# Sixteen starting places for the split weights of an input projection

## The chip, the cores and the metric

The kernel runs on one core of a Trainium2 chip. The metric is the device time of one execution, in microseconds (us). A core has a matrix engine (PE, whose weight loads the profile lists apart as PEld), three engines for elementwise work (DVE, ACT and POOL) and SP, which here only issues DMA transfers. Each engine takes its instructions in the order in which the program lists them and waits on semaphores for the others. Data for the engines lies in SBUF, a memory of 128 partitions, and a matrix product is summed in PSUM.

## The reference

One layer of a decoder trunk on x of 512 tokens by 4096 features, float32:

```python
h = rms_norm(x, norm_g)
q, k, v, z = split(h @ w_in + b_in)        # 4096, 512, 512 and 4096 columns
o = banded_sink_attention(q, k, v, sinks)  # 64 query heads, 8 key heads of 64, window of 128 tokens
x = x + (o * silu(z)) @ w_out + b_out
return rms_norm(x, final_g)
```

## The kernel before

Every float32 operand of a projection is split into two numbers, a high part that is rounded to a shorter form (`fp32r`) and the rest, and a product takes three matmuls: high by high, high by rest, rest by high. ACT makes the high part (`whi`) with a cast, and DVE the rest (`wlo`) with a subtraction (`split`, lines 141 to 145).

There are three stages.

1. The value projection. x is loaded, scaled and split into `xhi` and `xlo`, which stay in SBUF, and for each of 32 blocks of 128 features four blocks of tokens are multiplied with 512 columns of the value weights. x is the operand that is loaded into PE as weights here, `whi` and `wlo` stream past it. The last `LAST` = 3 blocks are held back and taken one token block after another, so that three pairs of split weights are in use at once until the end of the stage.
2. The input projection, with the attention laid between its matmuls. 68 column tiles (`NT`) of 128 output columns follow each other: per pair of key groups one tile of keys (name `None`), and then per group eight of `TILES`. A column tile has 8 chunks (`kc`), a chunk 4 blocks (`j`), a block 3 matmuls, so 96 matmuls of 512 columns. Here 128 columns of `whi` or `wlo` are loaded into PE and `xhi` or `xlo` stream past. One chunk is one buffer of `whi` and one of `wlo`, 512 columns each; `load_w` brings two chunks in one DMA of 512 KB. After each chunk, `tick` lets due pieces of attention follow: scores (`ps`), then the transposes of the probabilities (`pt`), then the product with the values (`po`). A *quad* is the attention of four query heads in four token blocks; there are 16 quads, each with four blocks of tokens.
3. The output projection, in 8 blocks of 512 columns, where the split gated output `gs` is loaded into PE and `whi` and `wlo` stream past it, and then the final norm.

`whi` and `wlo` have `WB` = 4 buffers each in all three stages. The cast of a chunk waits until PE has done with the chunk four before. PE's instructions are kept in the order in which the code gives them (`mm`, `tr`); those of the other engines are put into an order by a scheduler when the program is built.

What lies where in a partition: the buffers of `whi` and `wlo` are 2,048 bytes long, those of `xhi` and `xlo` 8,192 bytes with a block of 2,048 bytes each, and every one of them begins 128 bytes past a multiple of 512. Since a block of weights within a buffer begins at a multiple of 512 bytes too, the weights of any matmul of a projection lie at a multiple of 512 bytes from the x that streams past (distance 0 from here on, for all such multiples). `gs` of the output projection lies at distance 0 from `whi` as well. The buffers of the attention (`q`, `kh`, `vv`, `vw`, `wh`) begin 64 bytes past a multiple of 512.

## Time and profile before

| | |
|---|---|
| median of 2 runs | 2407.35 us (2406.91 to 2407.78) |
| the profiled execution | 2406.92 us |
| its span, first to last instruction | 2405.2 us |
| PE busy | 2392.2 us, 99% of the span |
| DVE, ACT, POOL busy | 58%, 41%, 14% |
| clock granted to PE, mean | 0.998 of full speed |

A row of the profile names the source line, the engine, the operation, and `out<-in` by the program's names. `acc<-xhi,wlo` on PE is a matmul into `acc` with x streaming and `wlo` loaded. A matmul row gives the start, which is measured, and a length, whose end is modelled; matmuls overlap, so that the spacing of starts is what a matmul costs.

### The profile page before, as it was taken

The numbers are of one execution on the slowest core, as the hardware profiler recorded it, in microseconds if no ns is written. First come the engines' busy times: TensorE is split into PE (matmuls) and PEld (weight loads), VectorE is DVE, ScalarE is ACT, GpSimd is POOL, SyncE is SP. The second block draws the span as 40 slices with busy tenths as digits, with TensorE's granted clock in tenths as the row PEclk, the third lists the DMA queues.
The fourth block names the chain that finished last, engine by engine and source line by source line (L and its number), as shares of the span: only waits on it lengthen the run. The fifth ranks groups of instructions, "written<-read, shape, count | busy, mean of one in ns | idle before, by whom it ended". The sixth has DMA issues, their size and how long they took to land.

```text
span 2405.2 us, 30234 instructions
## 1 busy us (share of the span) xinstructions
PE 2392.2 (99%) x10988; PEld 1991.1 (83%) x10988; DVE 1403.9 (58%) x2502; ACT 985.0 (41%) x2129; POOL 340.7 (14%) x472
## 2 busy tenths in 40 slices
PE   9999999999999999999999999999999999999998
PEld 7888888888888888888888888888888888888886
DVE  5446656555575564656656466565764664665565
ACT  6433433434343342433433334334444444444444
POOL 1101111121020121102102011111210110110110
PEclk9999999999999999999999999999999999999999
DMA  9633233233333323333233332334633433333334
GB/s 343 189 93 102 85 110 97 88 112 86 103 99 92 102 89 110 92 94 105 85 105 104 92 99 86 112 97 128 228 123 97 125 123 100 124 124 97 122 119 184
DMA packets 81077, 280.45 MB, mean 117 GB/s; under 512 B 10080, under 2 KB 10080, under 8 KB 80928
## 3 DMA queue, kind: packets, MB, share of 16 engines
q1 hardware_dynamic: 70176, 243.37, 32.7%
q0 software_dynamic: 10608, 34.88, 4.4%
q8 instruction: 86, 1.41, 0.2%
q14 instruction: 63, 0.52, 0.1%
q10 hardware_dynamic: 144, 0.28, 0.0%
HBM read 259.61 MB, written 18.88 MB: 116 GB/s over the span
## 4 chain that ended last, share of the span: by engine, by line
PE 99%; DMA 0%; DVE 0%; POOL 0%; ACT 0%; DVEq 0%; issue 0%; POOLq 0%
PE acc L112 94%; PE ps L112 2%; PE po L112 2%; PE pt L115 1%; DMA xraw<-in_x 0%; POOL wl L425 0%; POOL wh L425 0%; DVE y L688 0%; ACT xhi L241 0%; ACT y L712 0%; DVE xb L711 0%; DVEq L794 0%; DVE y L692 0%; POOL ww L425 0%; DVE y L678 0%
## 5 line engine op out<-in xcount | busy, mean ns | idle before, releaser
L144 DVE TENSOR_TENSOR wlo<-raw,whi 128x512 fp32r<-128x512 f32 x822 | 587.4, 716 | 760.2 <-ACT whi L143 751.5
L143 ACT CAST whi<-raw 128x512 fp32r<-128x512 f32 x821 | 510.7, 622 | 1204.1 <-PE acc L112 1148.3
L112 PE MATMUL acc<-xhi,wlo 128*128 128x512 f32 x2176 | 849.2, 390 | 0.0
L112 PE MATMUL acc<-xhi,whi 128*128 128x512 f32 x2176 | 848.6, 390 | 0.0
L112 PE MATMUL acc<-xlo,whi 128*128 128x512 f32 x2176 | 848.3, 390 | 0.0
L112 PE MATMUL acc<-whi,gs 128*128 128x512 f32 x1968 | 606.0, 389 | 0.0
L112 PEld LDWEIGHTS acc<-xhi,wlo 128*128 128x128 f32 x2176 | 408.4, 188 | 85.8
L112 PEld LDWEIGHTS acc<-xhi,whi 128*128 128x128 f32 x2176 | 409.1, 188 | 81.1
L112 PEld LDWEIGHTS acc<-xlo,whi 128*128 128x128 f32 x2176 | 408.4, 188 | 81.4
L112 PEld LDWEIGHTS acc<-whi,gs 128*128 128x128 f32 x1968 | 369.4, 188 | 76.7
L112 PE MATMUL acc<-wlo,gs 128*128 128x512 f32 x984 | 382.8, 389 | 0.0
L112 PEld LDWEIGHTS acc<-wlo,gs 128*128 128x128 f32 x984 | 184.7, 188 | 38.4
L144 DVE TENSOR_TENSOR gs<-g,gs 128x512 fp32r<-128x512 f32 x256 | 186.8, 770 | 0.7 <-ACT gs L143 0.7
L425 POOL TENSOR_SCALAR_AFFINE_SELECT ww<-wh 64x512 fp32r<-64x512 f32 x64 | 41.7, 651 | 881.7 <-ACT wh L421 881.7
L143 ACT CAST gs<-g 128x512 fp32r<-128x512 f32 x256 | 145.7, 616 | 1.7 <-PE acc L112 1.7
L497 DVE RECIPROCAL e<-e 128x128 f32<-128x128 f32 x128 | 120.6, 944 | 0.5
L399 ACT ACTIVATE prob<-ps,nm 128x128 f32<-128x128 f32 x256 | 90.4, 364 | 74.2 <-DVE nm L390 73.0
L704 POOL DMA_DIRECT2D xb<-in_x x32 | 17.3, 541 | 504.6 <-DVE y L714 430.8
L474 ACT COPY ot<-po 64x256 f32<-64x256 f32 x128 | 46.9, 367 | 56.8 <-DVE o L475 41.2
L475 DVE TENSOR_TENSOR o<-po,ot 64x256 f32<-64x256 f32 x128 | 52.8, 412 | 20.4 <-ACT ot L474 19.8
L348 DVE SCALAR_TENSOR_TENSOR q<-tmp,bcol,q 64x512 fp32r<-64x512 f32 x64 | 58.6, 916 | 7.2 <-ACT q L347 6.2
L274 DVE TENSOR_TENSOR tmp<-acc,rbc 128x512 f32<-128x512 f32 x37 | 25.6, 691 | 57.6 <-PE acc L112 57.6
(125 smaller groups left out, 1629.3 us busy)
## 6 DMA issues: line engine op xcount, KB each, us to landing
raw<-in_w_in SPq DMA_DIRECT2D x272, 512.0 KB, 3.6
raw<-in_w_out SPq DMA_DIRECT2D x128, 512.0 KB, 3.6
row<-in_x POOLq DMA_DIRECT2D x16, 512.0 KB, 6.5
gT<-o POOLq DMA_DIRECT2D x32, 256.0 KB, 2.3
g<-gT SPq DMA_DIRECT2D x16, 512.0 KB, 6.3
xb<-in_x POOLq DMA_DIRECT2D x32, 256.0 KB, 3.6
xraw<-in_xT SPq DMA_DIRECT2D x15, 512.0 KB, 7.1
raw<-in_w_v SPq DMA_DIRECT2D x15, 512.0 KB, 6.4
```

The source lines that it names most:

```text
L112: tc.keep_in_program_order(nc.tensor.matmul(*a, **k))
L115: tc.keep_in_program_order(nc.tensor.transpose(*a, **k))
L143: copy(hi, src),
L144: nc.vector.tensor_tensor(lo, src, hi.bitcast(F32), op=ALU.subtract),
L274: nc.vector.tensor_tensor(t, acc, rbc, op=ALU.mult)
L348: nc.vector.scalar_tensor_tensor(q2[other, :, h, :], tv[own], b[own], q2[own, :, h, :].bitcast(F32), op0=ALU.add, op1=ALU.subtract,)
L399: nc.scalar.activation(pr[:, u, a, :], ps[:, u, a, 0:P], AF.Exp, bias=nm[:, u, a:a + 1], scale=SCALE, accum_out=den[:, u, a:a + 1],)
L425: nc.gpsimd.affine_select(out=out, in_=src.bitcast(F32), fill=0.0, pattern=[[0, 8], [1 if own else -1, QH]], compare_op=ALU.is_ge if own e ...
L474: nc.scalar.copy(ot[own], pq[other, :, :, h, :])
L475: nc.vector.tensor_tensor(ov[own], pq[own, :, :, h, :], ot[own], op=ALU.add)
L497: nc.vector.reciprocal(c, c)
L704: nc.gpsimd.dma_start(xb, x[tb * P:(tb + 1) * P, cs])
```

## The change

The buffers of `whi` and `wlo` become longer by 128 columns (2,560 bytes), and each column tile but the last uses 512 columns that begin at one of sixteen places in them: 0, 4, 8, 12, 16, 24, and so on to 96 and 112 columns, in turn from tile to tile. In bytes the distance from x becomes 0, 16, 32, 48, 64, 96, 128, then by steps of 32 to 384, and 448, beyond a multiple of 512. The stages of the value projection and of the output projection, and the last column tile, keep place 0. So that the longer buffers fit, there are three of each in place of four, in all stages.

```diff
-WB = 4
+WB = 3
+
+PLACES = (0, 4, 8, 12, 16, 24, 32, 40, 48, 56, 64, 72, 80, 88, 96, 112)
...
+    place = [0]
...
     def split_w(raw, j, copy=nc.scalar.copy):
-        hi = wpool.tile([P, CW], F32R, name="whi", tag="whi", bufs=WB)
-        lo = wpool.tile([P, CW], F32R, name="wlo", tag="wlo", bufs=WB)
+        hi, lo = (
+            wpool.tile([P, CW + P], F32R, name=n, tag=n, bufs=WB)[:, place[0]:place[0] + CW]
+            for n in ("whi", "wlo")
+        )
         latest[1:] = split(raw[:, j], hi, lo, copy)
         return hi, lo
...
         for t, (g_, name) in enumerate(order):
             assert t == tile_no(g_, name)
+            place[0] = PLACES[t % len(PLACES)] if t < NT - 1 else 0
```

PE's instructions stand in the same order before and after. On the other engines the scheduler puts some of them elsewhere, because it reckons with three buffers. Lines of the new kernel are 2 to 7 further down.

On ACT, at the end of the value projection, the casts of the first chunks of the input projection stand ahead of a cast of the values, `vv`, that needs `vf`, which comes back from memory. Before:

```order
L241 ACTIVATE xhi_776<-xraw,gcol 128x512
L143 CAST whi<-raw 128x512
L241 ACTIVATE xhi_776<-xraw,gcol 128x512
L143 CAST whi<-raw 128x512 x6
L329 CAST vv<-vf 128x4x64
L143 CAST whi<-raw 128x512 x9
L316 ACTIVATE kh<-kf,bk 128x512
```

And now:

```order
L247 ACTIVATE xhi_776<-xraw,gcol 128x512
L145 CAST whi<-raw 128x512
L247 ACTIVATE xhi_776<-xraw,gcol 128x512
L145 CAST whi<-raw 128x512 x5
L335 CAST vv<-vf 128x4x64
L145 CAST whi<-raw 128x512 x8
L322 ACTIVATE kh<-kf,bk 128x512
```

Five casts of chunks stand ahead of `vv` in place of six: chunk 5 of the first column tile is now cast behind it.

On DVE, in the first quad, around the third of its four token blocks: `wl` is the rest of the transposed probabilities (which POOL then masks for PE), `e` a part of the gate's reciprocal, `o` a piece of attention output. Before:

```order
L408 TENSOR_SCALAR prob<-prob,den 128x128 x4
L144 TENSOR_TENSOR wlo<-raw,whi 128x512
L497 RECIPROCAL e<-e 128x128
L144 TENSOR_TENSOR wlo<-raw,whi 128x512
L497 RECIPROCAL e<-e 128x128
L475 TENSOR_TENSOR o<-po,ot 64x2x2x64
L144 TENSOR_TENSOR wlo<-raw,whi 128x512
L497 RECIPROCAL e<-e 128x128
L475 TENSOR_TENSOR o<-po,ot 64x2x2x64
L383 COPY_PREDICATED ps<-mask,ps 128x4x64
L422 TENSOR_TENSOR wl<-pt,wh 128x512
```

And now:

```order
L414 TENSOR_SCALAR prob<-prob,den 128x128 x4
L146 TENSOR_TENSOR wlo<-raw,whi 128x512 x2
L503 RECIPROCAL e<-e 128x128
L481 TENSOR_TENSOR o<-po,ot 64x2x2x64 x2
L146 TENSOR_TENSOR wlo<-raw,whi 128x512
L503 RECIPROCAL e<-e 128x128
L428 TENSOR_TENSOR wl<-pt,wh 128x512
L389 COPY_PREDICATED ps<-mask,ps 128x4x64
```

One reciprocal and the masking of the next scores, which stood ahead of `wl`, stand behind it now.

## Rows read from the trace of the kernel before

**Rows 1.** The page: busy time of the engines, their share and instructions.

```profile
PE 2392.2 (99%) x10988; PEld 1991.1 (83%) x10988; DVE 1403.9 (58%) x2502; ACT 985.0 (41%) x2129; POOL 340.7 (14%) x472
```

**Rows 2.** All waits of PE: for whom, us in total, times, longest.

```profile
PE idle L112 <- DVE zero L191: 1.3, 1, 1.3
PE po L112 <- POOL wl L425: 0.4, 1, 0.4
PE acc L112 <- ACT xhi L241: 0.3, 1, 0.3
```

**Rows 3.** Chain that ended last: the output projection (start us, us, what).

```profile
1697.77 696.38 PE acc L112 x3072
```

**Rows 4.** Timeline of PE and of its weight loads, plain column tile (start us, us).

```profile
500.55 0.39 PE L112 MATMUL acc<-xhi,wlo 128*128 128x512 f32 x1
500.55 0.19 PEld L112 LDWEIGHTS acc<-xhi,whi 128*128 128x128 f32 x1
500.78 0.39 PE L112 MATMUL acc<-xhi,whi 128*128 128x512 f32 x1
...
503.27 0.39 PE L112 MATMUL acc<-xhi,wlo 128*128 128x512 f32 x1
```

**Rows 5.** Timeline of PE, the last warm-up matmuls on 16-bit zeros.

```profile
4.23 0.81 PE L112 MATMUL idle<-zero 128*128 128x512 bf16 x3
4.88 0.59 PE L112 MATMUL idle<-zero 128*128 128x512 bf16 x2
```

**Rows 6.** Timeline of PE, first matmuls of a chunk behind a block of scores.

```profile
164.36 0.39 PE L112 MATMUL acc<-xhi,whi 128*128 128x512 f32 x1
...
165.06 0.39 PE L112 MATMUL acc<-xhi,whi 128*128 128x512 f32 x1
...
166.67 0.39 PE L112 MATMUL acc<-xlo,whi 128*128 128x512 f32 x1
...
167.12 0.39 PE L112 MATMUL acc<-xhi,whi 128*128 128x512 f32 x1
```

**Rows 7.** Timelines of PE and PEld, last matmul of a chunk ahead of scores.

```profile
163.46 0.39 PE L112 MATMUL acc<-xhi,wlo 128*128 128x512 f32 x1
163.46 0.41 PEld L112 LDWEIGHTS ps<-kh,q 128*128 128x128 f32 x2
163.68 0.30 PE L112 MATMUL ps<-kh,q 128*128 128x64 f32 x2
```

**Rows 8.** The page: groups of line 143 and 144 (mean ns, idle before, releaser).

```profile
L144 DVE TENSOR_TENSOR wlo<-raw,whi 128x512 fp32r<-128x512 f32 x822 | 587.4, 716 | 760.2 <-ACT whi L143 751.5
L143 ACT CAST whi<-raw 128x512 fp32r<-128x512 f32 x821 | 510.7, 622 | 1204.1 <-PE acc L112 1148.3
```

**Rows 9.** Timelines at the start of the input projection: PE, ACT, DVE.

```profile
92.96 0.39 PE L112 MATMUL acc<-xhi,whi 128*128 128x512 f32 x1
...
98.38 0.62 ACT L143 CAST whi<-raw 128x512 fp32r<-128x512 f32 x1 [2.10 <-PE acc L112]
105.02 0.41 ACT L329 CAST vv<-vf 128x256 fp32r<-128x256 f32 x1 [6.01 <-DMA vf<-vd]
105.33 1.83 ACT L143 CAST whi<-raw 128x512 fp32r<-128x512 f32 x3
109.26 0.62 ACT L143 CAST whi<-raw 128x512 fp32r<-128x512 f32 x1 [2.10 <-PE acc L112]
...
105.98 3.58 DVE L144 TENSOR_TENSOR wlo<-raw,whi 128x512 fp32r<-128x512 f32 x3
```

**Rows 10.** Timelines in a quad, third token block: DVE, POOL, PE.

```profile
288.72 0.94 DVE L497 RECIPROCAL e<-e 128x128 f32<-128x128 f32 x1
...
290.62 0.69 DVE L422 TENSOR_TENSOR wl<-pt,wh 128x512 fp32r<-128x512 f32 x1
...
292.71 1.17 POOL L425 TENSOR_SCALAR_AFFINE_SELECT wl<-wl 64x512 fp32r<-64x512 f32 x1
...
294.30 0.28 PE L112 MATMUL po<-wl,vv 128*128 128x256 f32 x1
```

## The prediction

> **What bounds the kernel now.** I began with the page: PE is busy for 99% of the span, no other engine for more than 58% [rows 1]. Busy alone proves little, since matmuls overlap, so I read PE's waits next: it waited three times, for 2.0 us in all [rows 2]. Nothing that feeds PE is late, and a change can only move the time through the cost of a matmul or by making PE wait where it doesn't now.

> The cost of a matmul is the spacing of starts. In a plain column tile, with no attention in it, twelve matmuls take 503.27 - 500.55 = 2.72 us, 226.7 ns each [rows 4]; over the whole output projection it is 696.38 / 3072 = 226.7 ns [rows 3]. The weights of the next matmul begin to load when the present one begins to stream (both at 500.55) and take 0.19 us [rows 4], so they are ready before it ends: the load is hidden, as far as time goes. Yet 226.7 ns isn't the least that 512 columns can take here. The last warm-up matmuls, also of 512 columns, but of 16-bit numbers, started (4.88 - 4.23) / 3 = 217 ns apart [rows 5]. So each matmul in fp32r carries some 10 ns more. Whether this has to do with where weights and x lie is what the change depends on.

> **The distances.** The input projection has 68 x 96 = 6528 matmuls. The place is 0 in tiles 0, 16, 32, 48, 64 and the last, so 62 tiles or 5952 matmuls get another distance. Between them the distances differ only below 512 bytes, and there every projection now has distance 0; the trace of before can't show the spacing at 16 or 32 bytes. It has one neighbouring case. The last matmul of a chunk ahead of a block of scores streams x while the weights of the scores are loaded, and these (`q`) begin 64 bytes past a multiple of 512 where x begins 128 past: the distance is -64, the same as 448, one of the sixteen. The load starts with that matmul (163.46), and the next matmul starts 163.68 - 163.46 = 0.22 us after it [rows 7], as at distance 0 to the resolution of the row. So one of the fifteen new places costs what place 0 costs, by this row.

> From both sides the cost of the other places is bounded by rows of other matmuls of this shape. Below: the warm-up's 217 ns, that is 10 ns less. Above: right behind a block of scores, where x and weights are at distance 0, the matmuls do not start 226.7 ns apart at once. From 164.36 to 166.67 there are ten, 231 ns each, the first three (to 165.06) 233 ns each; then two more to 167.12 take 0.45 us, which is the usual spacing again [rows 6]. The same instruction on the same addresses can thus cost some ns more, by how it meets the work ahead of it. I take 0, because the row with another distance [rows 7] is nearer to the question than rows with another type or another past. Both ends go into the range.

> [...]

> **Three buffers in place of four.** ACT spends most of its idle time ahead of a cast waiting for PE, that is for a free buffer [rows 8]. A cast now starts when the chunk four before is done, and three chunks of 12 x 226.7 ns = 2.72 us pass until its own turn, 8.16 us; with cast and subtraction (0.62 and 0.72 us [rows 8]) some 6.8 us are left, plus two matmuls for `wlo`. With three buffers the lead is 2.72 us shorter and 4 us are left. That hides it nearly everywhere. I looked for the places where something other than the buffer delays a chunk, and found two that matter.

> The first is the start of the input projection. ACT stands at `vv` until 105.02, when `vf` has come back from memory, after 6.01 us of idle time [rows 9]. Six chunks (0 to 5) were cast ahead of it; the order now has five there, because a sixth buffer isn't free yet. So chunk 5 is the first behind `vv`: cast from 105.33 to 105.95, and its subtraction, the first of three that start at 105.98 and take 3.58 us, ends at about 107.2 [rows 9]. PE begins chunk 5 at 92.96 + 5 x 2.72 = 106.56 and needs `wlo` two matmuls later, at 107.0. So PE waits some 0.2 us, once. If `vf` lands a microsecond later than it did, it waits 1.2 us. The hold of three blocks at the end of the value projection, with all three buffers taken, costs less: the first of them is free six matmuls (1.36 us) before the stage ends, and a cast of 0.62 us needs no more.

> The second is the third token block of each quad. POOL ends the mask of `wl` at 293.88, and PE uses it at 294.30: 0.42 us to spare [rows 10], in each of 16 quads. That mask waits for `wl` on DVE at 290.62, behind reciprocals of 0.94 us. In the new order `wl` stands ahead of one reciprocal and a masking that it stood behind, so the margin should rather grow. If a later `wlo` pushes it back by one reciprocal instead, PE waits 0.94 - 0.42 = 0.5 us in each quad, 8 us in all.

> What else moves is free of cost: SP's loads of w_in wait for raw buffers that come free a chunk later, and there are three of these with two chunks each, so loads still run six chunks ahead of casts. PE's own order is unchanged. Longer buffers change no instruction's size, and the 4 us of lead hide it if casts into odd places take longer.

> **The sum.** Profiled execution 2406.92 us (span 2405.2), 0 for the distances, 0.2 for chunk 5, 0 for the quads: 2407.1. The profiled execution is 0.4 under the median of the runs shown, so **2407.5 us**. About 2% (48 us) is what a measurement of this kernel can tell from no change.

> **Rivals.**

> *The distance frees the 10 ns* (faster). The load of the next weights and the streaming x would be in each other's way at distance 0, and at other distances not. For it: the 10 ns that fp32r matmuls carry, exactly the same in all plain stretches, all of which are at distance 0 [rows 3, 4]. Against it: distance -64 shows the usual 0.22 us [rows 7]. Price: 5952 x (226.7 - 217) = 58 us if all places gain, 2350; half of that, 2378, if half do.

> *The distance costs more* (slower). The places would shift the moment at which weights and x meet, as a block of scores does, and the spacing would stay where it is only passing now. For it: the spacing behind scores is not that of the steady run [rows 6], so something in PE depends on the moment. Against it: it comes back to 226.7 within ten matmuls by itself. Price: 5952 x (231 - 226.7) = 26 us, 2433; with 233 ns, 37 us, 2445. It decides from any place on at which a whole tile runs above 21.8 us (96 x 226.7 ns).

> *Three buffers are too few* (slower). The quads wait 0.5 us each and the start 1.2: 2416. For it: the 0.42 us of margin. Against it: the new order on DVE.

> That the change doesn't do what it says can be left aside: all buffers lie at the same remainder of 512, so each tile has one distance throughout.

> **How the numbers follow.** No effect of the distance, and at most a microsecond of waits (2406 to 2410): 0.66. Distance frees time, in whole or in part: 0.13. Distance costs time: 0.15. Three buffers too few: 0.06. The range: 2390 to 2435. Below it lies the first rival where it gains more than 3 ns per matmul (17 us), which I put at 0.09 of its 0.13; above it the second where it costs more than its mean price, 0.06. Faster by over 2% (under 2359) needs 8 ns of the 10 in every place: 0.05. Slower by over 2% (over 2455) needs 235 ns, more than any row for long: 0.05. Within 2%: 0.90.

> **What the profile of the changed kernel would show.** If I am right, every plain column tile takes 21.8 us whatever its place, and matmul starts are 0.227 us apart in each; PE's waits stay under 4 us, with one new one, for chunk 5 of the first tile. If a rival is right, the tiles differ by place, and those that share a place (16 tiles apart) agree. I would be wrong above all if places of 16 or 32 bytes, of which no row tells anything, run at another spacing than those of 64.

## The result, and the profile after

The changed kernel takes 2437.15 us (median of 2 runs, 2436.59 to 2437.72) against 2407.35: 1.0124 times as long, 95% interval 1.008 to 1.0167. The forecast was 2407.5 us with a range up to 2435. The time lies 2 us above the range and beside the price of the second rival (2433, or 2445). Its profiled execution took 2436.59 us, with a span of 2434.6 us where it was 2405.2.

The page, busy time of the engines, answers to [rows 1]: PE has 29.5 us more, the other engines nothing that could account for it.

```profile
PE 2421.7 (99%) x10988; PEld 1993.6 (82%) x10988; DVE 1404.8 (58%) x2502; ACT 982.2 (40%) x2129; POOL 334.0 (14%) x472
```

All waits of PE (us in total, times, longest), against [rows 2]: three, for 1.8 us in all. Waits of PE's weight loads are not in this view; two places where they are new, for 0.9 and 0.6 us, are described further down.

```profile
PE idle L114 <- DVE zero L197: 1.3, 1, 1.3
PE po L114 <- POOL wl L431: 0.3, 1, 0.3
PE acc L114 <- DVE part L662: 0.2, 1, 0.2
```

So the matmuls themselves cost more. Which ones is read from the page's groups of lines (busy us, mean ns of one, idle before): those that stream x past the weights have a longer modelled length than before, 395 ns in place of 390, and those of the output projection, with the same shape and type, have the same as before. Before:

```profile
L112 PE MATMUL acc<-xhi,whi 128*128 128x512 f32 x2176 | 848.6, 390 | 0.0
...
L112 PE MATMUL acc<-whi,gs 128*128 128x512 f32 x1968 | 606.0, 389 | 0.0
```

And now:

```profile
L114 PE MATMUL acc<-xhi,whi 128*128 128x512 f32 x2176 | 858.7, 395 | 0.0
...
L114 PE MATMUL acc<-whi,gs 128*128 128x512 f32 x1968 | 606.2, 389 | 0.0
```

The chain that ended last, at the start of the output projection, gives the stage (start us, us, what), to compare with [rows 3]:

```profile
1726.74 607.25 PE acc L114 x2679
```

The timeline of PE at the start of the input projection (93.56), and at the two ends of the first chunk of two column tiles, at 256 bytes (330.98) and at 32 bytes (523.57), answers to [rows 4]:

```profile
93.56 0.39 PE L114 MATMUL acc<-xhi,whi 128*128 128x512 f32 x1
...
330.98 0.39 PE L114 MATMUL acc<-xhi,whi 128*128 128x512 f32 x1
...
333.70 0.39 PE L114 MATMUL acc<-xhi,whi 128*128 128x512 f32 x1
...
523.57 0.40 PE L114 MATMUL acc<-xhi,whi 128*128 128x512 f32 x1
...
526.37 0.40 PE L114 MATMUL acc<-xhi,whi 128*128 128x512 f32 x1
```

Twelve matmuls take 333.70 - 330.98 = 2.72 us at 256 bytes and 526.37 - 523.57 = 2.80 us at 32 bytes: 226.7 and 233.3 ns each. The input projection begins at 93.56 and the output projection at 1726.74, 1633.2 us later; before it was 1697.77 - 92.96 = 1604.8 [rows 3, 9]. So 28.4 of the 29.4 us of span lie in the input projection, 0.6 before it and 0.4 behind it.

The view by windows, each window one column tile without attention, from its first matmul to that of the next tile (columns: window, its length, PE busy and instructions, granted clock of PE, DMA share, GB/s; a window also counts one to three instructions at its edges). The places are, in turn, 0, 16, 32, 256, 16 and 16 bytes:

```profile
93.56:115.34 21.78, 21.78 (x98) 1.00 0.51 182
115.34:137.10 21.76, 21.76 (x97) 1.00 0.39 124
137.10:159.50 22.40, 22.40 (x98) 1.00 0.29 91
330.98:352.75 21.77, 21.77 (x97) 1.00 0.34 97
501.17:523.57 22.40, 22.40 (x99) 1.00 0.38 119
1652.50:1674.26 21.76, 21.76 (x97) 1.00 0.30 98
```

These tiles of 96 matmuls have one of two lengths, 21.76 us (226.7 ns each) or 22.40 us (233.3 ns), at a granted clock of 1.00 in both. In tiles without attention, places 0 and 256 always have the short one, 32 always the long one, and 16 bytes had the short one in two tiles and the long one in another. Other places have other spacings. From the starts of all matmuls, the means of tiles without attention are 233 to 234 ns for 48, 64, 96, 160, 224, 288, 320 and 352 bytes, 232 or 233 for 128 and 384, 229 in one tile and 233 in another for 192, and 229 for 448. No place ran below 226.7.

### The profile page after: what moved, and what is told of

Its sections match the earlier page's. It is cut to its first block, busy times and chain, and to the rows that moved or that the text cites. A ratio compares the mean times of both kernels' runs of the same rounds, so it can differ in the third digit from the quotient of the medians.

```text
span 2434.6 us, 30333 instructions
## 1 busy us (share of the span) xinstructions
PE 2421.7 (99%) x10988; PEld 1993.6 (82%) x10988; DVE 1404.8 (58%) x2502; ACT 982.2 (40%) x2129; POOL 334.0 (14%) x472
## 4 chain that ended last, share of the span: by engine, by line
PE 98%; DVE 1%; DMA 0%; issue 0%; POOL 0%; ACT 0%; DVEq 0%; SPq 0%; POOLq 0%
PE acc L114 93%; PE ps L114 2%; PE po L114 2%; PE pt L117 1%; DMA g<-gT 0%; PE idle L114 0%; DVE xb L718 0%; DVE wlo L146 0%; DVE y L721 0%; DVE gs L146 0%; POOL wl L431 0%; POOL wh L431 0%; DVE y L695 0%; ACT y L719 0%; DVE xlo L248 0%
## 5 line engine op out<-in xcount | busy, mean ns | idle before, releaser
L114 PE MATMUL acc<-xhi,whi 128*128 128x512 f32 x2176 | 858.7, 395 | 0.0
L114 PE MATMUL acc<-xhi,wlo 128*128 128x512 f32 x2176 | 858.0, 394 | 0.0
L114 PE MATMUL acc<-xlo,whi 128*128 128x512 f32 x2176 | 857.5, 394 | 0.0
```

Of the source, the lines that this page charges most:

```text
L114: tc.keep_in_program_order(nc.tensor.matmul(*a, **k))
```

## The experiments

First the kernels with 4 or 10 executions, then those with one, which are read by the spacing in their tiles rather than by their time. "Before" is the kernel before on the same chip.

| kernel | us | before, or ratio (95% interval) |
|---|---|---|
| e1_place0 | 2408.27 | 1.0003 (0.9994 to 1.0013) |
| e2_place256 | 2408.21 | 1.0004 (0.9994 to 1.0013) |
| e4_both32 | 2408.49 | 1.0004 (0.9994 to 1.0014) |
| e3_place32 | 2445.12 | 1.0157 (1.0142 to 1.0172) |
| e7_lo32 | 2445.43 | 1.0158 (1.0143 to 1.0173) |
| e5_xpad32 | 2466.9 | 1.0247 (1.0232 to 1.0262) |
| e6_fine | 2433.51 | 2407.53 |
| e10_repeat | 2403.35 | 2407.53 |
| e11_pairs | 2441.98 | 2406.82 |
| e9_halves | 2478.31 | 2406.82 |
| e12_lengths | 2607.72 | 2406.78 |
| e13_twice | 2361.5 | 2408.08 |

**Is it the place at all?** Two kernels with the longer buffers, three of each, and one place for all tiles:

```diff
-PLACES = (0, 4, 8, 12, 16, 24, 32, 40, 48, 56, 64, 72, 80, 88, 96, 112)
+PLACES = (0,)     # e1_place0
+PLACES = (8,)     # e3_place32
```

> The three longer buffers stay, and every column tile uses place 0. Theory (the distance between the weights that are being loaded and the operand that streams decides a matmul's spacing; at 0 and 256 bytes 226.7 ns, elsewhere about 233.3): every plain column tile 21.8 us, about 2408.4 us, the 1 us over the kernel before being waits from three buffers. Rival A (where the weights themselves begin, whatever x does): the same. Rival B (three buffers and the order that follows from them cost the 30 us): about 2437 us.

> Every column tile but the last begins 32 bytes on (place 8). Theory and rival A: 67 x 96 matmuls x 6.7 ns = 43 us over e1_place0, about 2451 us, a plain tile 22.4 us. Rival B: about 2437 us, as the kernel with sixteen places.

With place 0 the time is that of before within its interval: buffers, their number and the new order on ACT and DVE are not the cause. With 32 bytes in every tile it is 2445.12; the span is 2443.1 - 2406.8 = 36.3 us longer than that of e1_place0. The expectation of 2451 was too high because it counted a surplus of 6.7 ns on all 6432 matmuls of 67 tiles, 43 us. By the starts in both traces, the matmuls in undisturbed stretches lose that much (6.6 ns each, 31.2 us), but those within twelve behind a block of attention, which pass through 231 to 233 ns before too [rows 6], lose 3.0 ns each, 5.0 us.

**The place or the distance?** A pad of 32 bytes ahead of x and `gs` moves them by 32 bytes. In e4_both32 the weights are moved with them, in e5_xpad32 they stay, so that all three stages are at a distance of 32:

```diff
+    pad = xg.tile([P, 8], F32, name="pad", tag="pad", bufs=1)
+    nc.gpsimd.memset(pad, 0.0)
...
-    place = [0]
+    place = [8]       # e4_both32, with PLACES = (8,) and for the last tile too
+    place = [0]       # e5_xpad32, with PLACES = (0,)
```

> Weights and x (and the split output gs) are all 32 bytes on, in all stages, so the distance is 0 again while nothing stands where it stood. Theory: about 2408.4 us, all stages at 226.7 ns. Rival A: every projection at 233.3 ns, 9984 x 6.7 ns = 66 us more, about 2475 us; or, if only whi and wlo count, about 2452 us.

> whi and wlo stay at place 0, and x and gs lie 32 bytes further on, so that all stages have a distance of 32 bytes. Theory: 9864 matmuls x 6.7 ns = 66 us over e1_place0, about 2474 us, in all three stages (there it is whi and wlo that stream past x or gs in two of them). Rival A: the input projection stays at 226.7 ns, and the other stages, where x or gs is loaded, cost 3456 x 6.7 ns = 23 us, about 2431 us; or 2408.4 us, if only whi and wlo count.

With both moved nothing is lost (2408.49 us against 2408.27 of e1_place0): it is the distance, not the address of either. With x alone moved all stages pay. The output projection, in which `gs` is loaded and the weights stream, the roles exchanged, has this line in the chain that ended last of e5_xpad32:

```profile
1738.07 716.14 PE acc L116 x3072
```

716.14 / 3072 = 233.1 ns, against 226.7 in [rows 3]. Expected were 2474. By the starts in the two traces, the three stages take 2.7, 36.4 and 19.3 us longer than in e1_place0: the first and the last about what 6.7 ns each would make, the input projection, with its stretches behind attention, 7 us less.

**Is it periodic?**

```diff
+PLACES = (64,)     # e2_place256
```

> Every column tile but the last begins 256 bytes on. Theory (what counts is the distance up to a multiple of 256 bytes): 226.7 ns in plain tiles, as e1_place0, about 2408.3 us. Rival (only 0 up to a multiple of 512 is good, and tiles 10, 26, 42, 58 of the sixteen-place kernel were lucky in what ran ahead of them): 233.3 ns, as e3_place32, about 2445 us.

256 bytes cost what 0 costs (2408.21 us against 2408.27 of e1_place0), in every tile. Then finer places, 0 to 28 bytes by 4, and around 256:

```diff
+PLACES = (0, 1, 2, 3, 4, 5, 6, 7, 60, 61, 62, 63, 64, 65, 66, 68)     # e6_fine
```

> The places become 0, 4, 8, 12, 16, 20, 24, 28 bytes and 240, 244, 248, 252, 256, 260, 264, 272 bytes. If pieces of 16 bytes are what meets, 4 to 12 bytes and 244 to 264 bytes run as 0 and 256, at 226.7 ns; if the exact address counts, all but 0 and 256 run at about 233.3 ns. Were a distance without any meeting to exist, one of them would run near 217 ns; I expect none. About 2425 to 2440 us.

The windows of e6_fine, one column tile each, at 4, 8, 244, 12, 248, 252, 252 and 244 bytes:

```profile
115.79:138.10 22.31, 22.31 (x98) 1.00 0.34 121
138.10:160.24 22.14, 22.14 (x97) 1.00 0.31 93
308.74:330.51 21.77, 21.77 (x98) 1.00 0.44 135
545.25:567.65 22.40, 22.40 (x97) 1.00 0.33 95
716.19:738.59 22.40, 22.40 (x99) 1.00 0.43 128
738.59:760.35 21.76, 21.76 (x97) 1.00 0.34 98
1123.92:1146.31 22.39, 22.39 (x98) 1.00 0.44 131
1457.17:1479.56 22.39, 22.39 (x97) 1.00 0.27 94
```

A step of 4 bytes, one column, already counts: 232.4 ns at 4 bytes, 230.7 at 8, 233.3 at 12. 260 and 264 bytes repeat the means of 4 and 8 to 0.1 ns, so 256 bytes are a period. 244 and 252 bytes have two steady spacings, 226.7 and 233.3 ns, like 16 bytes above; a tile without attention keeps one from beginning to end. Where attention lies between the chunks, the spacing can change there. At 16 bytes, the tile of the changed kernel that begins at 1266.04 us runs its first 24 matmuls at 226.7 ns and, behind a block of attention, the next 36 at 233.3; the tile of e6_fine that begins at 567.65 us changes from 233.3 to 226.7 behind one such block and back behind the next. So how a run of matmuls begins can settle which of the two it keeps; what about its beginning does so isn't shown.

**Does each load pay for its own distance?** `whi` at distance 0, `wlo` at 32 bytes, so that one load in three is displaced:

```diff
+PLACES = (8,)
...
-            wpool.tile([P, CW + P], F32R, name=n, tag=n, bufs=WB)[:, place[0]:place[0] + CW]
-            for n in ("whi", "wlo")
+            wpool.tile([P, CW + P], F32R, name=n, tag=n, bufs=WB)[:, p:p + CW]
+            for n, p in (("whi", 0), ("wlo", place[0]))
```

> whi stays at place 0 and wlo alone begins 32 bytes on, so one load in three is at another distance, the one that runs while xlo streams. If each matmul pays for its own distance: a third of 6.7 ns on the mean, 228.9 ns in plain tiles, about 2421 us, and the 6.7 ns stand behind one matmul in three. If it takes an undisturbed run at distance 0 to reach 226.7 ns (as the ten matmuls behind a block of scores suggest): 233 ns for all, about 2445 us.

It costs all that e3_place32 costs. The timeline of PE in a plain tile of e7_lo32:

```profile
116.77 0.40 PE L114 MATMUL acc<-xhi,whi 128*128 128x512 f32 x1
117.00 0.40 PE L114 MATMUL acc<-xlo,whi 128*128 128x512 f32 x1
117.24 0.39 PE L114 MATMUL acc<-xhi,wlo 128*128 128x512 f32 x1
117.47 0.40 PE L114 MATMUL acc<-xhi,whi 128*128 128x512 f32 x1
```

Three starts are 117.47 - 116.77 = 0.70 us apart, 233.3 ns each in the mean, where three at distance 0 take 0.68. The finer times of the trace repeat 232, 239 and 229 ns, the 239 in the matmul that streams `xlo`, under which `wlo` is loaded. None of the three runs at 226.7: one displaced load in three slows its neighbours too, so that no price for each load alone describes it; the spacing belongs to the run of matmuls.

**What must move?** In turn a usual tile, one whose 128 columns of weights are one column repeated, the same at 32 bytes, and one whose x is one column repeated:

```diff
+PLACES = (0, 0, 8, 0)
...
+            if mode[0] in (1, 2):
+                h, l = (w[:, 0:1].broadcast_to([P, P]) for w in (h, l))
+            if mode[0] == 3:
+                xhj, xlj = (w[:, 0:1].broadcast_to([P, S]) for w in (xhj, xlj))
...
+            mode[0] = t % 4 if t < NT - 1 else 0
```

> Four kinds of column tile in turn: as before at place 0; weights read from one column over and over (128 times the same address) at place 0; the same at place 8 (32 bytes); and x read from one column over and over, place 0. The products of three tiles in four are therefore others. If the time above 217 ns is the loads' reading of many pieces of SBUF beside the stream, the second and third kind run at about 217 ns, both alike, and the fourth too; if it is a price of fp32r matmuls wherever their data lie, all four run at 226.7 ns, and the third perhaps at 233 ns.

Windows of e10_repeat: repeated weights at place 0, then at 32 bytes, then repeated x.

```profile
493.48:515.72 22.24, 22.24 (x99) 1.00 0.36 121
515.72:537.96 22.24, 22.24 (x97) 1.00 0.41 116
537.96:558.68 20.72, 20.72 (x98) 1.00 0.31 101
```

Neither expectation held. Repeated weights run at 22.24 us / 96 = 231.7 ns at both places, slower than usual weights at place 0. With one column of x repeated a matmul takes 20.72 / 96 = 215.8 ns, 10.9 ns less than the usual 226.7: the 10 ns that I took for a possible collision in the first rival can go, but not by a distance.

**Two ideas of the mechanism that fell.** I supposed next that the stream of x and the load of weights pass over the 256 bytes at unequal pace, one overtaking the other, and that weights interleaved column by column (8 bytes from one to the next), or a shorter stream, would show it: interleaved weights would then run faster. No run shows the two paces. The rival was that a load costs what it costs now beside any stream that moves, or more.

```diff
+PLACES = (0, 4, 8, 12, 16, 20, 24, 28, 32, 36, 40, 44, 48, 52, 56, 60)
...
+            pairs = w[:, place[0]:place[0] + 2 * CW].rearrange("p (c i) -> p c i", i=2)
+            hi, lo = pairs[:, :, 0], pairs[:, :, 1]     # e11_pairs
```

> whi and wlo of a chunk lie in one buffer, column by column beside each other, in the input projection, so that a load of 128 weights reads every second number over 1,024 bytes; sixteen places, 0 to 240 bytes by 16, in turn; three buffers. [...] About 2350 us by the theory, 2410 to 2450 by the rival.

In tiles without attention, all sixteen places of e11_pairs ran at 230.0 to 233.5 ns, none faster than the 226.7 of usual weights at place 0, and the time, 2441.98 us, lies where the rival put it. The best of them by its mean, 112 bytes, in a window of one column tile (22.08 us / 96 = 230.0 ns):

```profile
645.68:667.76 22.08, 22.08 (x98) 1.00 0.34 96
```

In e9_halves each matmul becomes two of 256 columns, each with its own load; even tiles at place 0, odd ones at 32 bytes:

```diff
+PLACES = (0, 8)
...
+            for i in range(2):
+                s = slice(i * S // 2, (i + 1) * S // 2)
+                mm(acc[:, s], h, xhj[:, s], start=first and i == 0, stop=False)
+                mm(acc[:, s], h, xlj[:, s], start=False, stop=False)
+                mm(acc[:, s], l, xhj[:, s], start=False, stop=last and i == 1)
```

> Each matmul of the input projection is made as two of 256 columns, each with its own load, at place 0 in even and 32 bytes in odd column tiles. [...] Some 2500 to 2620 us.

Windows of e9_halves, place 0 and then 32 bytes, 192 matmuls each:

```profile
140.15:163.18 23.03, 23.03 (x194) 1.00 0.28 92
216.31:239.03 22.72, 22.72 (x195) 1.00 0.32 109
```

23.03 / 192 = 120.0 ns at place 0 and 22.72 / 192 = 118.3 ns at 32 bytes, both above half of what 512 columns take there (226.7 and 233.3). So the time doesn't go with the columns that stream alone; and 32 bytes cost less than place 0, where a price for each load would have made them cost more, as they do with 512 columns. What a distance costs thus depends on the length of the stream, and no price per load describes it. Both ideas, the overtaking and a price per load, fell. The expected 2500 to 2620 us rested on such a price, which no run shows; measured were 2478.31.

**Load or stream?** Tiles with shorter loads and with other streams:

```diff
+PLACES = (0, 0, 0, 0, 0, 0, 8, 0)
...
+            if m in (1, 2, 6) and inner:          # all but the first and last j
+                n = 32 if m == 2 else 64
+                h, l, acc = h[:, 0:n], l[:, 0:n], acc[0:n]
+            if m == 3:
+                xhj, xlj = (w[:, 0:32].unsqueeze(1).to_broadcast([P, S // 32, 32]) for w in (xhj, xlj))
...
+            if m == 4:
+                xhj, xlj = (w[:, 0:S // 2].unsqueeze(2).to_broadcast([P, S // 2, 2]) for w in (xhj, xlj))
...
+            if m == 5:                            # every second of 1,024 columns
+                xhj, xlj = (
+                    c[kc].rearrange("p j (s i) -> p j s i", i=2)[:, k:k + 2, :, 0] for c in (xh, xl)
+                )
...
+            if m == 7:
+                h, l = (xl[kc].rearrange("p j (s i) -> p (j s) i", i=16)[:, :, i] for i in (0, 0))
```

> All places are 0, but for tiles t with t % 8 = 6 (32 bytes), and the load or the stream is changed in seven tiles of eight, whose products are therefore others (t % 8 = 0 is the usual tile): 1 loads the first 64 columns of the weights in 94 of its 96 matmuls, 2 the first 32, 6 the first 64 at 32 bytes; 3 streams the first 32 columns of x sixteen times over, 4 the first 256 columns twice each, 5 every second column of 1,024; 7 loads every sixteenth of 2,048 columns of xlo as weights. [...] Second theory: a load costs a fixed price whatever its length. Then 226.7 ns in tiles 1 and 2 and 233.3 ns in tile 6. [...]

Windows of e12_lengths, in this order tiles of the kinds 1, 2, 3, 6, 7, 4, 0 and 5:

```profile
541.74:563.84 22.10, 22.10 (x99) 1.00 0.40 122
563.84:586.07 22.23, 22.23 (x97) 1.00 0.38 119
586.07:608.79 22.72, 22.72 (x97) 1.00 0.27 95
893.22:915.46 22.24, 22.24 (x98) 1.00 0.37 114
915.46:938.05 22.59, 22.59 (x97) 1.00 0.32 99
1034.43:1055.15 20.72, 20.72 (x98) 1.00 0.33 99
1150.96:1172.75 21.79, 21.79 (x98) 1.00 0.26 76
1480.64:1523.95 43.31, 43.31 (x97) 1.00 0.18 60
```

64 columns cost 22.10 / 96 = 230 ns, 32 columns 232, and 64 columns at 32 bytes 232. The fixed price of the second theory would have given 227, 227 and 233, and a price that goes with the columns loaded less than the 227.0 ns of the usual tile here (21.79 / 96) for the first two: neither describes it. A shorter load saves nothing. Weights gathered over 16 times the bytes (kind 7) cost 22.59 / 96 = 235.3 ns, 8.3 more than the usual tile. The stream is another matter. Every second column, 8 bytes from one to the next, takes 43.31 / 96 = 451 ns, twice the usual; each column twice takes 20.72 / 96 = 215.8 ns, as little as one column repeated. This fits a stream that is charged by the bytes that it passes over: 512 columns over 4,096 bytes take 451 ns, over 2,048 bytes 227 ns, over 1,024 bytes 215.8, beside the 217 ns of the 16-bit warm-up matmuls [rows 5], whose 512 columns are 1,024 bytes too. By that reading a stream of 4 bytes a column has next to nothing to spare. The number of different bytes is not what counts: the same 128 bytes sixteen times over (kind 3) cost 22.72 / 96 = 236.7 ns, more than the usual tile, and why more stays open.

**Does the distance act only where the stream has nothing to spare?** x streams as 256 columns, each twice, in three tiles of four, at 32, 96 and 352 bytes; the fourth is the usual one at 32:

```diff
-PLACES = (0, 4, 8, 12, 16, 24, 32, 40, 48, 56, 64, 72, 80, 88, 96, 112)
+PLACES = (8, 8, 24, 88)
...
+            if mode[0] in (1, 2, 3):
+                xhj, xlj = (w[:, 0:S // 2].unsqueeze(2).to_broadcast([P, S // 2, 2]) for w in (xhj, xlj))
+                acc = acc.rearrange("p (a b) -> p a b", b=2)
```

> In three column tiles of four x is streamed as its first 256 columns, each twice in a row, so that their products are others; they stand at 32, 96 and 352 bytes, and the fourth tile is the usual one at 32 bytes. Before this run, x read so took 215.8 ns at place 0, as little as x that repeats one column, and x of every second column took 452 ns, twice the usual: the stream of 512 columns of 4 bytes seems to use all that the path of the moving operand can read, and a load hurts it only for that reason. First theory: the distance acts only where the stream has no reads to spare. Then all three places run at 215.8 ns, 20.7 us a tile, as place 0 did, and the usual tile at 32 bytes stays at 233.3. The time would be about 2445 - 50 x 96 x 17.5 ns = 2361 us. Second theory: a load at a wrong distance holds the stream whatever its rate. Then the three stay 6 to 7 ns above place 0, at 222 to 223 ns, and the time is about 2395 us.

Windows of e13_twice: the usual tile at 32 bytes, then 32, 96 and 352 bytes with each column twice.

```profile
93.76:116.15 22.39, 22.39 (x97) 1.00 0.54 175
116.15:136.87 20.72, 20.72 (x97) 1.00 0.42 125
136.87:157.59 20.72, 20.72 (x97) 1.00 0.32 102
525.38:546.10 20.72, 20.72 (x97) 1.00 0.33 101
```

All three places run at 215.8 ns, the usual tile beside them at 233.3. The time is 2361.5 us, where the first theory said 2361 and the second 2395. With half the bytes to stream, none of the three distances costs anything; of the two theories the first is left.

## Why the prediction was wrong

**The distances: the step that failed.** The prediction took 0 for the other places "because the row with another distance [rows 7] is nearer to the question". That row is one matmul, whose load at -64 bytes ran behind a run at distance 0 and ahead of matmuls of another shape. e7_lo32 shows that the spacing belongs to a whole run, so one matmul could bear neither for nor against. 448 bytes, the same as -64, ran at 229 ns in whole tiles, 2 ns above place 0: the cheapest of the new places but 256 and some tiles at 16, and a surplus below the 0.01 us that the row resolves. So the term "0 for the distances" of the sum was mis-sized: it measured 28.4 us. [Rows 6] were the better rows: they show the very instruction at 231 and 233 ns, and most new places hold 232 to 234 ns throughout. I had set them aside as "another past", and gave the right rival 0.15.

**The second rival was right in kind, and near in size.** It said that the spacing "would stay where it is only passing now" and gave 26 us at 231 ns and 37 us at 233. Measured: 28.4 us in the input projection, 28.4 / 5952 = 4.8 ns per matmul. It lies between because places at 256 bytes and some tiles at 16 cost nothing and 448 little, and because the matmuls behind attention were already above 226.7. That this mean falls between the two prices, which came from ten matmuls at distance 0, is partly luck. Its mechanism, a shifted moment at which weights and x meet, is not shown; that the spacing can change behind a block of attention (e6_fine) speaks for it. What I did not foresee is that 256 bytes are a period, and that a place may have two spacings.

**The first rival** (the distance frees 10 ns) was wrong in its way and right in one number. 226.7 - 215.8 = 10.9 ns are there to be freed, but what frees them is a stream of fewer bytes (e10_repeat, e12_lengths, e13_twice), never a distance: 226.7 ns is the best of all places tried.

In time, 32 bytes alone make 37 us in the input projection (e3_place32, 2445.12 against 2408.27 of e1_place0) and 59 us in all stages (e5_xpad32, 2466.9).

**Three buffers.** The steps held where a term was large and missed small ones. The quads don't wait (one wait for `wl` of 0.3 us, 0.4 before). The wait of 0.2 us for chunk 5 didn't come: `vf` was there 2 us earlier, at 102.96 in place of 105.02 [rows 9], and the subtraction that was to be late began at 103.92, ahead of the chunk's start at 93.56 + 5 x 2.72 = 107.2. What the prediction called cheap, the hold of three blocks, costs 0.6 us, at its beginning and not at its end. Before, the last block of x was split on ACT and DVE by 84.51, ahead of the held blocks:

```profile
82.87 0.72 ACT L241 ACTIVATE xhi<-xraw,gcol 128x512 fp32r<-128x512 f32 x1
...
83.77 0.74 DVE L242 SCALAR_TENSOR_TENSOR xlo<-xraw,gcol,xhi 128x512 fp32r<-128x512 f32 x1
```

The timelines of ACT, DVE and PE's weight loads in the changed kernel:

```profile
84.99 0.62 ACT L145 CAST whi<-raw 128x512 fp32r<-128x512 f32 x1 [1.47 <-PE acc L114]
85.52 0.72 ACT L247 ACTIVATE xhi<-xraw,gcol 128x512 fp32r<-128x512 f32 x1
...
86.27 0.75 DVE L248 SCALAR_TENSOR_TENSOR xlo<-xraw,gcol,xhi 128x512 fp32r<-128x512 f32 x1
...
86.29 0.19 PEld L114 LDWEIGHTS acc<-whi,xhi 128*128 128x128 f32 x1 [0.40 <-ACT xhi L247]
...
87.08 0.19 PEld L114 LDWEIGHTS acc<-whi,xlo 128*128 128x128 f32 x1 [0.49 <-DVE xlo L248]
```

The held blocks begin at 84.79. The weights of the third of them can be cast only when the block ahead of the hold gives its buffer back, at 84.99, and the split of that block's x stands behind the cast on ACT and behind the subtraction on DVE. PE wants the block six matmuls after the hold began, and it is the loads of `xhi` and `xlo` into PE that come late. Another 0.4 us are lost at one place of the output projection, where a load waits 0.58 us for a `wlo` on DVE; of that the waits of PE show 0.2. With all that, e1_place0 measures the three buffers alone at 2408.27 us against 2407.56 of the kernel before beside it, 0.7 us, within its interval.

## What to carry to other kernels

Where PE bounds a kernel with 4-byte operands, in matmuls of 512 columns with 128 columns loaded, keep the weights and the operand that streams past them at a distance of a multiple of 256 bytes in the partition: 0 and 256 bytes ran at 226.7 ns here, and 32 bytes off cost 1.6 to 2.5% (at 256 columns 32 bytes were slightly better than 0, 118.3 against 120.0 ns, so other shapes want a run of their own). Any small buffer that a pool places ahead of them can shift them without a word in the code of the matmuls, as the pad of 32 bytes did in e5_xpad32. The spacing of matmuls should be read per tile over dozens of them, since a single matmul, or a mean over places, hides it. When the same instruction shows two spacings in one trace, as in [rows 6], the worse one may be what another layout makes permanent, and deserves more than a remark.

## What the runs showed of the hardware that was not expected

- A stream of 512 columns takes 215.8 ns over 1,024 bytes, 226.7 over 2,048 and 451 over 4,096 (e12_lengths): reading every second column of 4 bytes cost double.
- At the first of these the distance had no effect (20.72 us a tile at 32, 96 and 352 bytes, e13_twice).
- 16, 244 and 252 bytes have two steady spacings, 226.7 and 233.3 ns; a tile without attention keeps the one in which it begins, and behind a block of attention the spacing can change (226.7 to 233.3 ns in the tile of the changed kernel at 1266.04 us).
- Loading 64 or 32 columns of weights in place of 128 made a matmul no shorter but 3 to 5 ns longer (230.2 and 231.6 ns against 227.0, e12_lengths), and with 256 columns streaming 32 bytes were better than 0, 118.3 against 120.0 ns (e9_halves).
